# One weight sum of the block products made by an adding DMA, and the first weight tile of a stretch at 32 bytes

## The chip, the cores and the metric

The kernel runs on one core of a Trainium2 chip. The metric is the device time of one execution in microseconds (us). The kernel before takes 2368.86 us, the median of three runs (2367.31 to 2369.78). The engines are named as in the profile: PE (TensorE, matmuls), PEld (its weight loads), DVE (VectorE), ACT (ScalarE), POOL (GpSimd) and SP (SyncE, which here only issues DMAs).

## The reference

Two layers of an encoder trunk on 512 tokens of width 1024, all in fp32. Each layer is a gated feed-forward block, a mixer (two attentions and a pooling branch, gated and summed), and a second feed-forward block; each is normalised and modulated before and added to `x` after:

```python
def swiglu(h, w_gate, w_up, w_down):
    return (jax.nn.silu(h @ w_gate) * (h @ w_up)) @ w_down

for l in range(DEPTH):                       # DEPTH = 2
    mod = (c_act @ w_ada[l] + b_ada[l]).reshape(B, N_MOD, D_MODEL)
    h = modulate(rms_norm(x, norm_gain[l, 0]), mod[:, 0], mod[:, 1])
    x = x + 0.5 * mod[:, 2][:, None, :] * swiglu(h, ffn_w_gate[l, 0], ffn_w_up[l, 0], ffn_w_down[l, 0])
    ...                                      # the mixer, then the second swiglu
```

The hidden width D_FF is 2816, that is 22 column tiles of 128. The change lies in `h @ w_gate` and `h @ w_up` of the four feed-forward blocks.

## The kernel before

**Precision.** Each fp32 operand is split into a high part of type fp32r and the low rest. A product of two tiles is three matmuls: high by high, high by low, low by high. ACT casts the high part, DVE subtracts to get the low part (`split_to`, L417 and L418; `wchunk`, L310 and L312). The activations h lie transposed in `hhi` and `hlo`, 8 tiles of 128 rows by 512 tokens each.

**A feed-forward block** (`Ffn.run`, L629) goes through its 22 column tiles in three parts of 6, 8 and 8. A part first makes its activations (gate and up products, silu, multiplication), then multiplies them with the rows of `w_down` (`k_outer`, L421). Some column tiles of the first part are done directly, with matmuls of 512 columns (L140 to L142). All others are done in pairs by `seven` (L541), once for gate and once for up.

**`seven`** multiplies the 1024 rows and two column tiles of weights with all tokens as a 2 by 2 block product with seven multiplications instead of eight. Source 0 holds the weight blocks A11 and A12, source 1 holds A21 and A22. It forms four weight sums on DVE, each 128x512 per partition:

- S1 = A21 + A22 (L556), S3 = A11 - A21 (L557)
- S2 = S1 - A11 (L558), S4 = A12 - S2 (L559)

The matching activation sums T1 to T4 are made once for each feed-forward block (`Blocks`). The seven products, in the order in which PE makes them, are A11 B11, A12 B21, S2 T2, S1 T1, S3 T3, S4 B22 and A22 T4. Each is four tiles of three matmuls of 256 columns (`add_product`, L149 to L151), 84 matmuls for a call. Between them ACT copies the accumulators out of PSUM (L572 to L580) and DVE adds them up. The last product may start only after the copy at L580. There are 70 calls, in 11 stretches: three of two calls and eight of eight calls. Before each stretch stand matmuls of 512 columns.

**Where the data lies.** Raw weights are loaded by SP into `raw`, which has two buffers of 512 KB: both are taken by one call, and the loads of the next call wait until DVE has read them. Split weights go into `w` (three buffers) and, for the sums, `ptb` (two buffers). The unsplit sums and the evacuated products `c` take turns in `v2` (four buffers), which at other times takes rows of `w_ada`. `pta` (one buffer) serves the mixer alone. `duo` (L69) gives the place of a split weight inside its tile: `WIDE` = 0 for matmuls of 512 columns, `NARROW` = 16 floats, or 64 bytes, for those of 256. In the program's memory layout the tiles `w`, `b`, `hhi` and `hlo` start at multiples of 128 bytes, the tiles `ptb` 64 bytes past one.

**Halves-wise stages.** The last `k_outer` of each feed-forward block and of each mixer works on token halves, so its matmuls have 256 columns too (L428); its weights are placed at `NARROW` (L447). There are six such stages.

**Order.** The program is written in one order per engine by a planner, from a cost model and the order of the source; each engine then works strictly in order. Modulation work (`mod_step`, `mod_dot`) is slipped in by `side_work`, which `seven` calls ahead of each of its loads.

Of the kernel before, what the change touches and what calls it, by code (L numbers as in the profile page):

```python
# [15 lines left out]
F32 = mybir.dt.float32  # L16
# [3 lines left out]
ALU = mybir.AluOpType  # L20
# [20 lines left out]
def encoder_kernel(tc, xT, c, w_ada, b_ada, gains, w_gate, w_up, w_down, w_qkv, w_f, w_ubg,  # L41
# [22 lines left out]
    def st(shape, dt, tag, bufs):  # L64
        return sb.tile(shape, dt, tag=tag, bufs=bufs, name=nm(tag))

    WIDE, NARROW = 0, 16

    def duo(shape, tag="w", place=WIDE):  # L69

# [214 lines left out]
    def side_work(side=True):  # L285
        mod_flush()
        if quiet[0] > 0:
            quiet[0] -= 1
            if quiet[0] == 0:
                gate.clear()  # L290
        elif side and in_ffn[0] and mod_tag[0] != "raw":
            mod_credit[0] += MOD_RATE[0]
            while mod_credit[0] >= 1.0:
                mod_credit[0] -= 1.0
                mod_pop()

    def wchunk(src, shape, side=True, spare=None, lo_eng=None, place=WIDE):
        lo_eng = lo_eng or nc.vector
        side_work(side)
        raw = st([P] + list(shape), F32, *(("b", NB) if spare else ("raw", NRAW)))  # L300
        last["dma"] = nc.sync.dma_start(raw, src).ins
        if spare == "ptb":
            hi, lo = duo(shape, "ptb")
        elif spare == "b":
            hi = st([P] + list(shape), F32R, "b", NB)
            lo = st([P] + list(shape), F32R, "b", NB)
        else:
            hi, lo = duo(shape, "w", place)
        with behind("scalar"):
            nc.scalar.copy(hi, raw)  # L310
        with behind("vector"):
            lo_eng.tensor_tensor(lo, raw, hi.bitcast(F32), op=ALU.subtract)  # L312
        return hi, lo
# [107 lines left out]
    def k_outer(chunk_src, nch, lhs_rhs, before_last=None):  # L421

        if before_last is None:
            parts, nheld = [(None, slice(0, T), [acc() for _ in range(4)])], 2
        else:
            parts = [(hs, slice(hs * HALF, (hs + 1) * HALF), [b((P, HALF)) for _ in range(4)])  # L428
                     for hs, b in enumerate((mmt, acc))]
            nheld = 3  # L430

        def go(part, j, chunks):
            _, cols, accs = part
            for c, hi, lo in chunks:
                for kk in range(2):
                    a, b, x, y = lhs_rhs(hi[:, kk, :], lo[:, kk, :], 2 * c + kk, j)
                    triple(accs[j], a, b, x[:, cols], y[:, cols], start=(c == 0 and kk == 0),
                           stop=(c == nch - 1 and kk == 1))

        held = []  # L440
        for c in range(nch):
            if before_last is not None:
                if c == nch - 2:
                    quiet[0] = 8
                    before_last()
                quiet[0] = 8
            hi, lo = wchunk(chunk_src(c), (2, T), place=WIDE if before_last is None else NARROW)  # L447
            if c < nch - nheld:
                for part in parts:
                    for j in range(4):  # L450
                        go(part, j, [(c, hi, lo)])
            else:
                held.append((c, hi, lo))
        if before_last is not None:
            quiet[0] = 5
        for part in parts:
            for j in range(4):
                go(part, j, held[:-2])
            for j in range(4):
                go(part, j, held[-2:])  # L460
                yield j, part[0], part[2][j]
# [23 lines left out]
    def minus(o, a, b):  # L485
        nc.vector.tensor_tensor(o, a, b, op=ALU.subtract)  # L486
# [51 lines left out]
            q0, cols = {"T1": (0, FIRST), "T3": (0, SECOND), "T4": (2, FIRST), "T2": (2, SECOND)}[name]  # L538
            return [tuple(part[:, k % 2, cols] for part in self.parts[q0 + k // 2]) for k in range(4)]

    def seven(srcs, blocks, bank):  # L541

        raws = []
        for src in srcs:
            side_work()
            raw = st([P, KD, P], F32, "raw", NRAW)
            last["dma"] = nc.sync.dma_start(raw, src).ins
            raws.append(raw)
        tens = lambda o, a, b, op: nc.vector.tensor_tensor(o, a, b, op=op)
        a11, a12, a21, a22 = raws[0][:, :4], raws[0][:, 4:], raws[1][:, :4], raws[1][:, 4:]  # L550
        ah, al = duo((KD, P), "w", NARROW)
        split_to(ah, al, raws[0])
        bh, bl = duo((4, P), "w", NARROW)
        split_to(bh, bl, a22)
        s12, s34 = st([P, 2, 4, P], F32, "v2", 4), st([P, 2, 4, P], F32, "v2", 4)
        tens(s12[:, 0], a21, a22, ALU.add)  # L556
        minus(s34[:, 0], a11, a21)  # L557
        minus(s12[:, 1], s12[:, 0], a11)  # L558
        minus(s34[:, 1], a12, s12[:, 1])  # L559
        pair12, pair34 = duo((2, 4, P), "ptb"), duo((2, 4, P), "ptb")  # L560
        split_to(*pair12, s12)
        split_to(*pair34, s34)
        lefts = {"A11": [(ah[:, k], al[:, k]) for k in range(4)],
                 "A12": [(ah[:, 4 + k], al[:, 4 + k]) for k in range(4)],
                 "A22": [(bh[:, k], bl[:, k]) for k in range(4)]}
        for name, pair, i in (("S1", pair12, 0), ("S2", pair12, 1), ("S3", pair34, 0), ("S4", pair34, 1)):
            lefts[name] = [(pair[0][:, i, k], pair[1][:, i, k]) for k in range(4)]
        x, y, w = bank((P, HALF)), bank((P, HALF)), bank((P, HALF))
        c = st([P, 4, HALF], F32, "v2", 4)
        go = lambda o, left, right, start: add_product(o, lefts[left], blocks.operand(right), start)  # L570
        go(x, "A11", "B11", True)
        nc.scalar.copy(c[:, 0], x)  # L572
        go(y, "A12", "B21", True)
        tens(c[:, 0], y, c[:, 0], ALU.add)
        go(x, "S2", "T2", False)
        nc.scalar.copy(c[:, 1], x)
        go(w, "S1", "T1", True)
        nc.scalar.copy(c[:, 2], w)
        go(x, "S3", "T3", False)
        nc.scalar.copy(c[:, 3], x)  # L580
        go(w, "S4", "B22", False)
        tens(c[:, 1], w, c[:, 1], ALU.add)
        tens(c[:, 3], c[:, 2], c[:, 3], ALU.add)
        go(x, "A22", "T4", False)
        return [[c[:, 0:2].rearrange("p a t -> p (a t)")], [x, c[:, 3]]]
# [10 lines left out]
    class Ffn:  # L596
# [32 lines left out]
        def run(self, nxt):  # L629
# [4 lines left out]
            for part, (f0, nf) in enumerate(parts):  # L634
# [40 lines left out]
                    n += 1  # L675
                if not opening:
                    blocks.finish()
                while n < nf:
                    both = [apply(p, AF.Silu)
                            for p in seven([w_gate[l, s, f0 + n + i] for i in range(2)], blocks, acc)]  # L680
                    ups = seven([w_up[l, s, f0 + n + i] for i in range(2)], blocks, mmt)
                    for i, sg in enumerate(both):
                        acts.append(self.act(n + i, None, ups[i], sg))
                    n += 2
# [646 lines left out]
```

## Time and profile before

| | |
|---|---|
| median of three runs | 2368.86 us |
| the profiled execution's own time | 2370.22 us |
| its span (first to last instruction) | 2368.4 us |
| PE busy | 2335.2 us (99%) |
| DVE busy | 1770.8 us (75%) |
| ACT busy | 1197.2 us (51%) |
| POOL busy | 326.4 us (14%) |
| HBM read | 312.16 MB, 134 GB/s with what is written |

A row of a timeline has the start, the duration, the engine, the line, the operation, the tiles (written <- read), the shape and a count; in square brackets the idle time of the engine before it and what ended that. A row of a group has the count, then busy time and mean duration in ns, then the idle time before and who ended it. A row of a window has its length, then the busy time of each engine with the number of instructions that touch it, the granted clock, the share of time in which the DMA engines were busy, and GB/s. Matmuls are pipelined, so one matmul's duration is longer than the step from its start to the start of the next; the pace is read from the starts.

### The profile page before, as it was taken

The numbers are of one execution on the slowest core, as the hardware profiler recorded it, in microseconds if no ns is written. First come the engines' busy times: TensorE is split into PE (matmuls) and PEld (weight loads), VectorE is DVE, ScalarE is ACT, GpSimd is POOL, SyncE is SP. The second block draws the span as 40 slices with busy tenths as digits, with TensorE's granted clock in tenths as the row PEclk, the third lists the DMA queues.
The fourth block names the chain that finished last, engine by engine and source line by source line (L and its number), as shares of the span: only waits on it lengthen the run. The fifth ranks groups of instructions, "written<-read, shape, count | busy, mean of one in ns | idle before, by whom it ended". The sixth has DMA issues, their size and how long they took to land.

```text
span 2368.4 us, 37435 instructions
## 1 busy us (share of the span) xinstructions
PE 2335.2 (99%) x14322; PEld 2075.8 (88%) x14322; DVE 1770.8 (75%) x3147; ACT 1197.2 (51%) x2097; POOL 326.4 (14%) x433
## 2 busy tenths in 40 slices
PE   7999999999999999999999999999999999999999
PEld 5898998878888898989999989888788888999898
DVE  8887866787686577878687878677866855878583
ACT  5353555676632353635553536456765324636262
POOL 3000011244411100000100000112543211000000
PEclk9999999999999999999999999999999999999999
DMA  8535342333355524353415353533333654143233
GB/s 292 182 107 187 101 167 88 105 99 110 122 199 202 188 71 161 116 187 99 152 63 178 101 185 107 187 107 99 99 122 106 221 199 167 63 142 108 98 100 107
DMA packets 117976, 325.18 MB, mean 137 GB/s; under 512 B 11650, under 2 KB 13826, under 8 KB 117796
## 3 DMA queue, kind: packets, MB, share of 16 engines
q1 hardware_dynamic: 115106, 314.38, 39.9%
q0 software_dynamic: 2688, 8.39, 1.2%
q8 instruction: 113, 1.85, 0.3%
q14 instruction: 67, 0.55, 0.1%
q10 hardware_dynamic: 2, 0.00, 0.0%
HBM read 312.16 MB, written 6.38 MB: 134 GB/s over the span
## 4 chain that ended last, share of the span: by engine, by line
PE 85%; DVE 9%; ACT 3%; DMA 2%; issue 2%; SPq 0%; ACTq 0%; DVEq 0%; POOL 0%; POOLq 0%
PE acc L140 16%; PE acc L142 16%; PE acc L141 16%; PE mm L151 4%; PE mm L149 4%; PE mm L150 4%; PE acc L149 4%; PE acc L151 4%; PE acc L150 4%; PE mm L140 3%; PE mm L142 3%; PE mm L141 3%; PE mm L1020 1%; DVE w L418 1%; DVE v L486 1%
## 5 line engine op out<-in xcount | busy, mean ns | idle before, releaser
L312 DVE TENSOR_TENSOR w<-raw,w 128x1024 fp32r<-128x1024 f32 x247 | 313.2, 1271 | 161.6 <-ACT w L310 161.3
L310 ACT CAST w<-raw 128x1024 fp32r<-128x1024 f32 (+1 forms) x255 | 264.3, 1040 | 273.4 <-PE acc L142 187.5
L140 PE MATMUL acc<-b,w 128*128 128x512 f32 (+1 forms) x960 | 359.8, 375 | 0.0
L141 PE MATMUL acc<-b,w 128*128 128x512 f32 (+1 forms) x960 | 356.3, 371 | 0.0
L142 PE MATMUL acc<-b,w 128*128 128x512 f32 (+1 forms) x960 | 356.1, 371 | 0.0
L142 PEld LDWEIGHTS acc<-b,w 128*128 128x128 f32 x960 | 180.4, 188 | 31.6
L140 PEld LDWEIGHTS acc<-b,w 128*128 128x128 f32 x960 | 180.3, 188 | 30.3
L141 PEld LDWEIGHTS acc<-b,w 128*128 128x128 f32 x960 | 180.6, 188 | 29.8
L417 ACT CAST ptb<-v 128x1024 fp32r<-128x1024 f32 x140 | 146.6, 1050 | 100.8 <-DVE v L486 62.0
L418 DVE TENSOR_TENSOR ptb<-v,ptb 128x1024 fp32r<-128x1024 f32 x140 | 170.7, 1222 | 33.2 <-ACT ptb L417 32.7
L140 PE MATMUL acc<-hhi,w 128*128 128x512 f32 x480 | 191.9, 401 | 2.4 <-ACT hhi L747 1.7
L142 PE MATMUL acc<-hhi,w 128*128 128x512 f32 x480 | 188.8, 393 | 2.6 <-DVE w L312 2.6
L141 PE MATMUL acc<-hlo,w 128*128 128x512 f32 x480 | 188.7, 393 | 0.5 <-DVE hlo L750 0.5
L417 ACT CAST w<-raw 128x1024 fp32r<-128x1024 f32 (+1 forms) x140 | 116.5, 832 | 122.1 <-PE acc L142 56.2
L418 DVE TENSOR_TENSOR w<-raw,w 128x1024 fp32r<-128x1024 f32 (+1 forms) x140 | 133.1, 950 | 13.0 <-ACT w L417 13.0
L140 PE MATMUL acc<-w,hhi 128*128 128x512 f32 x336 | 138.7, 414 | 0.9 <-ACT t L849 0.9
L142 PE MATMUL acc<-w,hlo 128*128 128x512 f32 x336 | 131.9, 392 | 0.0
L141 PE MATMUL acc<-w,hhi 128*128 128x512 f32 x336 | 131.6, 392 | 0.0
L227 DVE CUSTOM_DVE_ANT_0 v<-v,b,badac 128x1024 f32<-128x1024 f32 x87 | 116.8, 1352 | 10.1 <-DMA v<-in_w_ada_dram 10.1
L149 PE MATMUL acc<-b,ptb 128*128 128x256 f32 x420 | 118.3, 282 | 0.0
L150 PE MATMUL acc<-b,ptb 128*128 128x256 f32 x420 | 117.8, 280 | 0.0
L151 PE MATMUL acc<-b,ptb 128*128 128x256 f32 x420 | 117.7, 280 | 0.0
(312 smaller groups left out, 6583.7 us busy)
## 6 DMA issues: line engine op xcount, KB each, us to landing
raw<-in_w_down_dram SPq DMA_DIRECT2D x88, 512.0 KB, 4.1
v<-in_w_ada_dram SPq DMA_DIRECT2D x87, 512.0 KB, 5.1
raw<-in_w_up_dram SPq DMA_DIRECT2D x82, 512.0 KB, 3.6
raw<-in_w_gate_dram SPq DMA_DIRECT2D x79, 512.0 KB, 3.6
b<-in_w_ada_dram SPq DMA_DIRECT2D x57, 512.0 KB, 4.7
raw<-in_w_ubg_dram SPq DMA_DIRECT2D x56, 512.0 KB, 3.6
raw<-in_w_qkv_dram SPq DMA_DIRECT2D x42, 512.0 KB, 3.7
raw<-in_w_branch_dram SPq DMA_DIRECT2D x24, 512.0 KB, 3.7
```

The lines of the kernel that those rows point to most:

```text
L140: mm(o, lh, rh, start=start, stop=False)
L141: mm(o, lh, rl, start=False, stop=False)
L142: mm(o, ll, rh, start=False, stop=stop)
L149: mm(o, lh, rh, start=start and k == 0, stop=False, skip_group_check=True)
L150: mm(o, lh, rl, start=False, stop=False, skip_group_check=True)
L151: mm(o, ll, rh, start=False, stop=k == 3, skip_group_check=True)
L227: dot = nc.vector.tensor_tensor_reduce(out=raw, in0=raw, in1=silc[0], scale=1.0, scalar=badac[:, l, j, d:d + 1], op0=ALU.mult, op1=ALU.add ...
L310: nc.scalar.copy(hi, raw)
L312: lo_eng.tensor_tensor(lo, raw, hi.bitcast(F32), op=ALU.subtract)
L417: nc.scalar.copy(hi, src)
L418: nc.vector.tensor_tensor(lo, src, hi.bitcast(F32), op=ALU.subtract)
L486: nc.vector.tensor_tensor(o, a, b, op=ALU.subtract)
```

## The change

In `seven`:

- A21 is no longer loaded into `raw`. SP loads it straight into the place of S1, in a `v2` buffer (256 KB), and an adding DMA from POOL's queue then adds A22 to it there (256 KB). The addition on DVE goes. With `s34` gone from `v2`, the sums S1, S2 of successive calls alternate with the products `c`.
- SP then loads the top tile (A11, A12; 512 KB) and A22 alone (256 KB) into `raw`.
- S3 is formed as A22 - S2, which is the same as A11 - A21, after S2 instead of before it.
- S3 and S4 lie in `pta` instead of `v2`.

Placement: the first weight tile of a stretch (the split A11, A12 of its first gate call) and the first weight chunk of each halves-wise stage stand at `ENTRY` = 8 floats, or 32 bytes, instead of 64 bytes.

```diff
-    WIDE, NARROW = 0, 16
+    WIDE, ENTRY, NARROW = 0, 8, 16
...
-            hi, lo = wchunk(chunk_src(c), (2, T), place=WIDE if before_last is None else NARROW)
+            hi, lo = wchunk(chunk_src(c), (2, T), place=WIDE if before_last is None else NARROW if c else ENTRY)
...
-    def seven(srcs, blocks, bank):
-
-        raws = []
-        for src in srcs:
-            side_work()
-            raw = st([P, KD, P], F32, "raw", NRAW)
-            last["dma"] = nc.sync.dma_start(raw, src).ins
-            raws.append(raw)
+    def seven(srcs, blocks, bank, place=NARROW):
+
+        top, low = srcs
+        s12, s34 = st([P, 2, 4, P], F32, "v2", 4), st([P, 2, 4, P], F32, "pta", 1)
+        nc.sync.dma_start(s12[:, 0], low[:, :4])
+        nc.gpsimd.dma_start(s12[:, 0], low[:, 4:], accum_op=ALU.add)
+        side_work()
+        r0 = st([P, KD, P], F32, "raw", NRAW)
+        last["dma"] = nc.sync.dma_start(r0, top).ins
+        side_work()
+        a22 = st([P, 4, P], F32, "raw", NRAW)
+        last["dma"] = nc.sync.dma_start(a22, low[:, 4:]).ins
         tens = lambda o, a, b, op: nc.vector.tensor_tensor(o, a, b, op=op)
-        a11, a12, a21, a22 = raws[0][:, :4], raws[0][:, 4:], raws[1][:, :4], raws[1][:, 4:]
-        ah, al = duo((KD, P), "w", NARROW)
-        split_to(ah, al, raws[0])
+        a11, a12 = r0[:, :4], r0[:, 4:]
+        ah, al = duo((KD, P), "w", place)
+        split_to(ah, al, r0)
         bh, bl = duo((4, P), "w", NARROW)
         split_to(bh, bl, a22)
-        s12, s34 = st([P, 2, 4, P], F32, "v2", 4), st([P, 2, 4, P], F32, "v2", 4)
-        tens(s12[:, 0], a21, a22, ALU.add)
-        minus(s34[:, 0], a11, a21)
         minus(s12[:, 1], s12[:, 0], a11)
+        minus(s34[:, 0], a22, s12[:, 1])
         minus(s34[:, 1], a12, s12[:, 1])
...
+                place = ENTRY
                 while n < nf:
                     both = [apply(p, AF.Silu)
-                            for p in seven([w_gate[l, s, f0 + n + i] for i in range(2)], blocks, acc)]
+                            for p in seven([w_gate[l, s, f0 + n + i] for i in range(2)], blocks, acc, place)]
+                    place = NARROW
                     ups = seven([w_up[l, s, f0 + n + i] for i in range(2)], blocks, mmt)
```

## The prediction

> **What bounds the kernel now.** I read the page first (busy time, clock, chain), then the exact windows of the block products, then single matmul starts in order of time, then the groups with their waits.
>
> ```profile
> span 2368.4 us, 37435 instructions
> ...
> PE 2335.2 (99%) x14322; PEld 2075.8 (88%) x14322; DVE 1770.8 (75%) x3147; ACT 1197.2 (51%) x2097; POOL 326.4 (14%) x433
> ...
> PEclk9999999999999999999999999999999999999999
> ...
> PE 85%; DVE 9%; ACT 3%; DMA 2%; issue 2%; SPq 0%; ACTq 0%; DVEq 0%; POOL 0%; POOLq 0%
> ```
>
> TensorE is busy for 99% of the span at the full granted clock and carries 85% of the chain. Work taken from another engine pays only where TensorE waits for it or runs at a slower pace. The change touches two kinds of stage: the 70 calls of `seven` (84 matmuls of 256 columns each) and the six halves-wise outer products.
>
> ```profile
> core 0: us, PE busy (x) PEld busy (x) DVE busy (x) ACT busy (x) POOL busy (x), PEclk, DMA share, GB/s
> 123.62:202.81 79.19, 78.95 (x674) 78.75 (x672) 69.50 (x105) 46.64 (x80) 0.00 (x0) 1.00 0.42 133
> ...
> 1290.48:1370.65 80.17, 79.08 (x674) 78.59 (x672) 69.00 (x103) 46.22 (x80) 0.00 (x0) 1.00 0.41 130
> ...
> sum 695.24, PE 689.72 PEld 686.73 DVE 597.36 ACT 401.50 POOL 0.00; mean PE 62.70 PEld 62.43 DVE 54.30 ACT 36.50 POOL 0.00
> ```
>
> These windows run from the first block matmul of each of the 11 stretches to the first matmul behind it. Together the 70 calls take 695.24 us, 29% of the span. VectorE is busy for 597.36 us of that, 86%.
>
> The pace inside a stretch has two values. The next rows are the first matmul of a call and of the call after it, early in a stretch and late in the same stretch:
>
> ```profile
> 246.35 0.28 PE L149 MATMUL acc<-hhi,w 128*128 128x256 f32 x1
> 256.25 0.28 PE L149 MATMUL mm<-hhi,w 128*128 128x256 f32 x1
> 295.91 0.28 PE L149 MATMUL mm<-hhi,w 128*128 128x256 f32 x1
> 305.43 0.28 PE L149 MATMUL acc<-hhi,w 128*128 128x256 f32 x1
> ```
>
> A call takes 9.90 us early and 9.52 us late: 117.9 and 113.3 ns per matmul, for the same 84 matmuls on the same kinds of tiles at the same clock. Neither contains a wait. So a call can run 4% faster with no instruction less. What lies between the two is a stall. The largest kind, later in the same stretch:
>
> ```profile
> 313.06 0.69 DVE L486 TENSOR_TENSOR v<-raw,v 128x512 f32<-128x512 f32 x1
> 313.11 1.05 ACT L417 CAST ptb<-v 128x1024 fp32r<-128x1024 f32 x1 [1.62 <-DVE v L486]
> 313.53 0.28 PE L151 MATMUL acc<-hhi,ptb 128*128 128x256 f32 x1
> 314.06 0.37 ACT L580 COPY v<-acc 128x256 f32<-128x256 f32 x1
> 314.48 0.38 PE L149 MATMUL acc<-b,w 128*128 128x256 f32 x1 [0.68 <-ACT v L580]
> ```
>
> The seventh product may not start before ScalarE has copied the accumulator (L580). ScalarE stands in order behind the cast of the next call's first weight sums, which waited 1.62 us for VectorE. Two matmul starts lie 0.95 us apart instead of 0.11.
>
> **The change, part by part.** First the two limits of what the block products can give. At 9.90 us with no stall the 70 calls take 693.0 us, at 9.52 us 666.4 us. Today's 695.24 is 2.2 above the first, because what the stalls cost and what the faster pace behind them saves nearly cancel. The second is 28.8 us away.
>
> *The VectorE addition that goes.* Before, A21+A22 is the instruction of the first row; the second is the cast that waits for VectorE:
>
> ```profile
> L549 DVE TENSOR_TENSOR v<-raw 128x512 f32<-128x512 f32 x70 | 48.2, 689 | 61.3 <-DMA raw<-in_w_gate_dram 58.5 <-DMA raw<-in_w_up_dram 2.7
> L417 ACT CAST ptb<-v 128x1024 fp32r<-128x1024 f32 x140 | 146.6, 1050 | 100.8 <-DVE v L486 62.0 <-ACT v L580 15.4 <-PE mm L151 11.9
> ```
>
> It takes 0.689 us x 70 = 48.2 us, and VectorE stands idle for another 61.3 us before it, nearly all until the second raw tile has landed. Afterwards S2 = sum - A11 needs only the first raw tile and the sum made by DMA. The remaining three VectorE subtractions are as many as before, 128x512 each (S3 reads A22 and S2 in place of A11 and A21), so 0 for them. The cast at 313.11 could start at least 0.69 us sooner, and up to 0.69 + 61.3/35 = 2.4 us sooner in a gate call, where the landing is waited for. The stall above, 0.95 - 0.11 = 0.84 us, lies between these two. I take it that half of the stall time goes; what is left I set at 4.5 us for all 70 calls (about 0.4 us in 11 of them), with 0 and 10 us as ends.
>
> *The transfers that come.* Per call: a plain 256 KB load on SP, an adding 256 KB load on POOL's queue behind it, the 512 KB top tile, a 256 KB load of A22; 1.25 MB where there was 1 MB. No adding DMA is in the trace. The nearest rows:
>
> ```profile
> raw<-in_w_gate_dram SPq DMA_DIRECT2D x79, 512.0 KB, 3.6
> x_dram<-xv POOLq DMA_DIRECT2D x8, 512.0 KB, 3.1
> strip<-in_rel_dram SPq DMA_DIRECT2D x16, 256.0 KB, 2.6
> b<-in_w_qkv_dram SPq DMA_DIRECT2D x6, 512.0 KB, 7.1
> raw<-in_w_down_dram SPq DMA_DIRECT2D x88, 512.0 KB, 4.1
> ...
> L1176 POOL DMA_DIRECT2D x_dram<-xv x8: 561/572/751, 343.1 to 1542.6; - x8
> ```
>
> Low end: it lands like a plain 256 KB load, 2.6 us. High end: like the slowest 512 KB row, 7.1 us, since it moves its bytes both in and out. I take 4, nearer the low end because the POOL-issued row of twice its size takes 3.1. With its forerunner and the issue on POOL the chain is 2.6 + 0.57 + 4 = 7.2 us; at the high end 4.1 (the w_down loads' median landing) + 0.75 + 7.1 = 12.0. Its cover:
>
> ```profile
> 294.13 1.23 DVE L418 TENSOR_TENSOR ptb<-v,ptb 128x1024 fp32r<-128x1024 f32 x1 [0.44 <-ACT ptb L417]
> 301.81 1.62 SPq L547 DMA_DIRECT2D raw<-in_w_up_dram  x2
> 311.14 0.68 DVE L549 TENSOR_TENSOR v<-raw 128x512 f32<-128x512 f32 x1
> ```
>
> The call whose sum VectorE forms at 311.14 has the slot that the call two before it gives up at 294.13 + 1.23 = 295.36. In SP's queue its first load stands ahead of the raw tiles issued at 301.81, so it can leave at 295.4 and the sum is whole at 302.6, at worst 307.4, against a need at 311.1. Cost 0, with 3.7 us to spare at the high end. POOL is idle in all eleven windows (POOL 0.00 in the sum), so nothing stands before or behind the DMA in its queue. The extra 0.25 MB fits a stage whose DMA engines are busy for 0.40 of the time. S3 and S4 now lie in a tile with one buffer (`pta`); its next writer comes one call, 9.5 us, later. Cost 0.
>
> *The first tile of a stretch at 32 bytes.* It moves no instruction. That the place of a weight tile matters is in the trace. Weights from `b` tiles stand at multiples of 128 bytes, from `ptb` and narrow `w` tiles 64 bytes past one:
>
> ```profile
> 862.87 0.29 PE L141 MATMUL mm<-hlo,b 128*128 128x256 f32 x1
> ...
> 863.79 0.28 PE L140 MATMUL mm<-hhi,ptb 128*128 128x256 f32 x1
> ...
> 864.13 0.28 PE L142 MATMUL mm<-hhi,b 128*128 128x256 f32 x1
> ...
> 866.29 0.28 PE L142 MATMUL mm<-hhi,b 128*128 128x256 f32 x1
> ...
> 2034.34 0.28 PE L141 MATMUL mm<-hlo,b 128*128 128x256 f32 x1
> 2034.46 0.28 PE L141 MATMUL mm<-hlo,ptb 128*128 128x256 f32 x1
> ...
> 2035.63 0.28 PE L142 MATMUL mm<-hhi,b 128*128 128x256 f32 x1
> ```
>
> Three steps from `ptb` take 0.34 us, 113 ns each; eighteen from `b` take 2.16, 120 each. The `ptb` tiles at 863.79 came after `b` tiles (862.87) and ran at 113; at 2034.46 the same switch left them at 1.17/10 = 117. So 64-byte tiles keep one of two paces, and a tile at another place, or a stall, can flip it. Every stretch is entered from 512-column tiles at 0 straight into tiles at 64 and starts at 117.9. With 24 matmuls at 32 bytes between, the pace may flip at the entry. Best case: all 70 calls at 113.3. Worst: the tile itself runs at 120 like `b` and nothing flips: 11 x 24 x 2 ns = 0.5 us lost. I take the flip, at a price of 11 x 24 x 6.7 ns (120 against 113.3) = 1.8 us for its own matmuls, because a switch of places flipped it at 863 and stalls flip it in the calls.
>
> The halves-wise stages get the same entry tile:
>
> ```profile
> 825.26:841.50 16.24, 16.24 (x139) 1.00 0.33 98
> ...
> 1515.80:1533.72 17.92, 16.75 (x139) 1.00 0.45 147
> ...
> 2342.25:2364.75 22.50, 22.50 (x193) 1.00 0.23 71
> ...
> sum 105.50, PE 104.33; mean PE 17.39
> ```
>
> Their six windows hold 5 x 138 + 191 = 881 matmuls. Without the 1.7 us that the row of 1515.80 has over its like, they take 103.8 at 117.9; at 113.3 it is 99.8: 4.0 less.
>
> Sum against the profiled execution's own 2370.22: -28.8 + 4.5 + 1.8 - 4.0 = -26.5, so 2343.7. That execution lies 1.4 above the median of 2368.86, so the median becomes about **2342**.
>
> **Rivals.** *Entry without effect.* The stalls go, but with them the faster pace that followed them. Then 693.0 + at most 2 in the calls: -2.2 to 0, 2367 to 2369. For it: each of the eleven entries now starts at the slow pace, and 2034.46 stayed there. Against it: the flip at 863. The Trainium skill ("SBUF — State Buffer", "Who interferes with whom") gives TensorE two independent read ports, for moving operand and weights, and says it never waits for anyone; by that a tile's place could not matter and this rival would be certain. The rows at 113, 118 and 120 ns speak against so strict a reading.
>
> *Flip that doesn't last.* The stretches start fast, but remaining stalls in gate calls flip some back. If half the calls stay slow, half of 28.8 + 4.0 is lost: about 2355. For it: VectorE has 597.36 - 48.2 = 549 us to do in 666.4, still 82%.
>
> *The transfers get in each other's way: slower.* Three loads on SP and one on POOL share the queues; if the 512 KB tile lands behind the new 256 KB pieces, VectorE's wait of 61.3 us grows by up to 2.6 us in 35 gate calls, 91 us, while it is spared 48.2. In proportion the stalls go from some 10 us (a dozen like the one shown) to 17, with the entry tile without effect: 693.0 + 17 against 695.24, and 3 us at the eleven starts, where modulation rows load beside: +18, about 2387. At a milder 1.5 us it is even; it decides from there. For it: b<-in_w_qkv at 7.1 us for 512 KB shows what crowding does. Against it: a DMA share of 0.40 and the 3.7 us to spare.
>
> The Trainium skill ("SBUF — State Buffer", "SBUF: two separate sides") warns that a GpSimd-issued DMA starves while VectorE runs a two-port instruction, and, by inference, excepts the two-input kind that fills these stages. If it starved all the same, by one 1.23 us instruction per DMA, the chain of 12.0 would be 13.2, still inside the 15.7 from 295.4 to 311.1.
>
> **How the numbers follow.** Forecast 0.52 (2334 to 2350), flip that doesn't last 0.13, no effect 0.20, in each other's way 0.15. 0.2% of the time, 4.7 us, is about what a measurement of this kernel can tell from no change: faster is the first two and a little of the third, 0.66; same the rest of the third, 0.19; slower 0.15. The range must leave out no more than 2 in 10: low end 2334 (all gains, no stall left, some 34 less), high end 2371, which takes in the third case and leaves the fourth out.
>
> **What would show it.** Right: the eleven windows sum to about 673 us, calls of 9.52 us from the first of a stretch on, the idle time before VectorE's first subtraction of a call well under 61.3 us, L580 waits under 2 us. Wrong: calls of 9.9 us at the start of a stretch (entry), a VectorE subtraction that waits for POOL's DMA (chain too slow), or the raw loads of w_gate landing later than 3.6 us (crowding).

## The result, and the profile after

The changed kernel takes **2474.01 us** (median of four runs, 2473.56 to 2482.07) against 2368.32 us of the kernel before on the same chip: a ratio of **1.0452** (95% interval 1.0439 to 1.0466), 105.7 us slower. The forecast was 2342 us. The profiled execution took 2474.18 us. In `after`, `seven` begins at L541; the load of A21 is L545, the adding DMA L546, the top tile L549, A22 L552, the copies out of PSUM L574 to L582. S2, S3 and S4 all go through the helper `minus` (L486).

From the page of the kernel after (span, busy time, bytes, chain of waits):

```profile
span 2472.4 us, 37580 instructions
...
PE 2356.6 (95%) x14322; PEld 2088.0 (84%) x14322; DVE 1727.8 (70%) x3077; ACT 1195.4 (48%) x2097; POOL 388.2 (16%) x503
...
HBM read 330.51 MB, written 6.38 MB: 136 GB/s over the span
...
PE 63%; DMA 16%; DVE 12%; ACT 5%; issue 3%; SPq 0%; POOLq 0%; POOL 0%; ACTq 0%; DVEq 0%
```

VectorE has lost 43 us of work, as intended, but DMA, 2% of the chain before, now carries 16% of it. The windows of the eleven stretches (length, then busy time by engine, granted clock, DMA share, GB/s; the second of the eight long ones, the first short one, the sum):

```profile
260.71:356.46 95.75, 83.04 (x673) 81.46 (x672) 64.00 (x99) 46.23 (x80) 6.05 (x7) 0.95 0.44 122
924.34:943.50 19.16, 19.16 (x170) 19.16 (x168) 15.06 (x24) 9.97 (x18) 0.89 (x1) 1.00 0.55 168
...
sum 800.94, PE 712.96 PEld 700.90 DVE 554.78 ACT 399.94 POOL 51.80; mean PE 64.81 PEld 63.72 DVE 50.43 ACT 36.36 POOL 4.71
```

800.94 - 695.24 = 105.70 us: the 70 calls hold the whole loss. TensorE is idle for 88 us of them (5.5 before). A short stretch of two calls can still be free of stalls: 19.16 us, which is 9.64 for the first call and 9.52 for the second. So the entry tile does what was forecast, and the loss grows with the length of a stretch. The group that waits:

```profile
L149 PE MATMUL mm<-b,ptb 128*128 128x256 f32 x420 | 126.3, 301 | 61.0 <-ACT v L574 50.9
L486 DVE TENSOR_TENSOR v<-v,raw 128x512 f32<-128x512 f32 x70 | 48.4, 692 | 178.9 <-DMA v<-in_w_up_dram 91.9
```

The first row is the start of each tile of the third to fifth products in half of the calls; TensorE waits 61.0 us before it, 50.9 of them for the copy at L574. The second row is S2 = sum - A11. VectorE stands idle for 178.9 us before it, nearly all until the sum has landed. Followed through one call, in the timelines of SP, POOL and VectorE, in order of time:

```profile
298.01 0.33 SPq L549 DMA_DIRECT2D raw<-in_w_gate_dram  x1
298.91 0.33 SPq L552 DMA_DIRECT2D raw<-in_w_gate_dram  x1
299.29 0.42 SPq L545 DMA_DIRECT2D v<-in_w_gate_dram  x1
303.50 0.86 POOL L546 DMA_DIRECT2D v<-in_w_gate_dram  x1 [10.41 <-DMA v<-in_w_gate_dram]
307.67 0.69 DVE L486 TENSOR_TENSOR v<-v,raw 128x512 f32<-128x512 f32 x1 [3.13 <-DMA v<-in_w_gate_dram]
308.40 0.69 DVE L486 TENSOR_TENSOR pta<-raw,v 128x512 f32<-128x512 f32 x1
309.15 0.33 SPq L549 DMA_DIRECT2D raw<-in_w_up_dram  x1
309.34 0.68 DVE L486 TENSOR_TENSOR pta<-raw,v 128x512 f32<-128x512 f32 x1
310.05 0.33 SPq L552 DMA_DIRECT2D raw<-in_w_up_dram  x1
310.43 0.42 SPq L545 DMA_DIRECT2D v<-in_w_up_dram  x1
```

This is **a loop**. On SP the load of A21 stands behind the top tile and A22 of its own call. It lands and POOL issues the adding DMA 4.21 us later; S2 starts 4.17 us after that. S3 gives up the raw buffer of A22 at 309.09 and S4 that of the top tile at 310.02; only then can SP issue the next two raw loads, and the next A21 behind them, at 310.43. One turn takes 310.43 - 299.29 = 11.14 us, and TensorE needs 9.52. This turn is one of the quicker ones: within the eight long stretches the issues of A21 lie 10.1 to 13.5 us apart, with a median of 11.6. In a stretch of eight calls TensorE catches up with the loop in the second call and waits in nearly every call from then on.

What that does on TensorE, in the call that uses the sum of 307.67 (timelines of PE and ACT):

```profile
310.67 0.28 PE L151 MATMUL acc<-hhi,w 128*128 128x256 f32 x1
312.12 0.62 ACT L417 CAST b<-t 128x512 fp32r<-128x512 f32 x1 [0.94 <-DVE t L626]
312.65 0.37 ACT L574 COPY v<-acc 128x256 f32<-128x256 f32 x1
313.07 0.54 PE L149 MATMUL acc<-b,ptb 128*128 128x256 f32 x1 [2.12 <-ACT v L574]
313.40 0.42 PE L150 MATMUL acc<-b,ptb 128*128 128x256 f32 x1
313.62 0.42 PE L151 MATMUL acc<-b,ptb 128*128 128x256 f32 x1
```

The third product may not start before the copy at L574, which stands on ScalarE behind casts that waited for VectorE, which had waited for the sum. And behind the wait TensorE does not resume at its pace: the next steps are 0.22 us instead of 0.11. In 14 of the 70 calls such steps of 213 ns follow, 208 of them when the matmul starts are counted: 208 x 0.1 us, some 21 us.

### The profile page after: what moved, and what is told of

It reads as the page before. It is cut to its first block, busy times and chain, and to the rows that moved or that the text cites. A ratio compares the mean times of both kernels' runs of the same rounds, so it can differ in the third digit from the quotient of the medians.

```text
span 2472.4 us, 37580 instructions
## 1 busy us (share of the span) xinstructions
PE 2356.6 (95%) x14322; PEld 2088.0 (84%) x14322; DVE 1727.8 (70%) x3077; ACT 1195.4 (48%) x2097; POOL 388.2 (16%) x503
## 4 chain that ended last, share of the span: by engine, by line
PE 63%; DMA 16%; DVE 12%; ACT 5%; issue 3%; SPq 0%; POOLq 0%; POOL 0%; ACTq 0%; DVEq 0%
PE acc L140 15%; PE acc L142 15%; PE acc L141 15%; DMA v<-in_w_up_dram 7%; DMA v<-in_w_gate_dram 4%; PE mm L142 3%; PE mm L140 3%; PE mm L141 3%; DVE pta L486 2%; DMA raw<-in_w_gate_dram 2%; PE mm L149 2%; PE mm L151 2%; PE mm L150 2%; DVE v L486 2%; DMA raw<-in_w_up_dram 1%
## 5 line engine op out<-in xcount | busy, mean ns | idle before, releaser
L149 PE MATMUL mm<-b,ptb 128*128 128x256 f32 x420 | 126.3, 301 | 61.0 <-ACT v L574 50.9
L486 DVE TENSOR_TENSOR v<-v,raw 128x512 f32<-128x512 f32 x70 | 48.4, 692 | 178.9 <-DMA v<-in_w_up_dram 91.9
L149 PE MATMUL acc<-b,ptb 128*128 128x256 f32 x420 | 124.2, 296 | 27.0 <-ACT v L574 26.7
L149 PEld LDWEIGHTS mm<-b,ptb 128*128 128x128 f32 x420 | 84.4, 201 | 69.3 <-ACT v L574 57.4
L417 ACT CAST ptb<-v 128x1024 fp32r<-128x1024 f32 x70 | 73.6, 1051 | 132.4 <-DVE v L486 132.4
L467 DVE SCALAR_TENSOR_TENSOR xv<-acc,badac,xv 128x512 f32<-128x512 f32 (+1 forms) x112 | 77.2, 690 | 68.9 <-PE acc L142 68.9
```

The lines of the kernel that those rows point to most:

```text
L149: mm(o, lh, rh, start=start and k == 0, stop=False, skip_group_check=True)
L417: nc.scalar.copy(hi, src)
L467: nc.vector.scalar_tensor_tensor(x, acc_j, gate, x, op0=ALU.mult, op1=ALU.add)
```

## The experiments

Calls is the sum of the eleven windows in the profiled execution (in bound_after other matmuls stand between the block products, and the sum is that of the pieces). Each ratio is to the kernel before as it ran beside that kernel, with medians from 2367.09 to 2368.78 us. The table is followed by the edits, in the order in which they were run.

| kernel | us | ratio to before (95%) | calls, us |
|---|---|---|---|
| before | 2368.32 | 1 | 695.24 |
| the change | 2474.01 | 1.0452 (1.0439 to 1.0466) | 800.94 |
| sum_first | 2402.32 | 1.0136 (1.0085 to 1.0187) | 727.64 |
| entry_only | 2362.18 | 0.9973 (0.9952 to 0.9994) | 687.52 |
| dma_only | 2482.22 | 1.0468 (1.0408 to 1.0529) | 808.52 |
| no_second | 2342.44 | 0.9892 (0.9867 to 0.9918) | 669.23 |
| plain_second | 2417.43 | 1.0206 (1.0186 to 1.0227) | 743.18 |
| sum_first_late_act | 2369.22 | 1.0005 (0.9995 to 1.0014) | 692.78 |
| entry_copy_first | 2362.20 | 0.9973 (0.9963 to 0.9983) | 691.65 |
| early_after | 2471.99 | 1.0439 (1.0423 to 1.0455) | 794.14 |
| early_64 | 2473.43 | 1.0438 (1.0421 to 1.0456) | 797.57 |
| early_vec | 2582.36 | 1.0905 (1.0888 to 1.0921) | 910.60 |
| pool_add | 2364.81 | 0.9985 (0.9976 to 0.9994) | 691.63 |
| entry_pool_sum | 2387.10 | 1.0071 (1.0059 to 1.0084) | 711.27 |
| sum_ahead | 2440.03 | 1.0306 (1.0292 to 1.0320) | 770.83 |
| sum_ahead_64 | 2446.73 | 1.0329 (1.0314 to 1.0343) | 771.76 |
| **bound_ahead** | **2347.83** | **0.9914 (0.9899 to 0.9928)** | 673.56 |
| bound_after | 2461.04 | 1.0394 (1.0376 to 1.0411) | 781.71 |
| bound_ahead_64 | 2366.37 | 0.9995 (0.9985 to 1.0005) | 688.02 |

**sum_first**: the A21 load goes ahead of the raw loads on SP.

```diff
-        nc.sync.dma_start(s12[:, 0], low[:, :4])
+        half = nc.sync.dma_start(s12[:, 0], low[:, :4]).ins
...
+        with tc.issue_after(half):          # the same for a22
             last["dma"] = nc.sync.dma_start(r0, top).ins
```

> The changed kernel with one thing ordered otherwise: on SP the load of A21 into the place of S1 is issued ahead of the two raw loads of its own call (in the changed kernel the planner put it behind them). All the work is the same. Theory (a loop through the DMAs: raw buffers free, r0 and A22 issued, only then A21, 3.6 to 5 us to land, then the adding DMA of 4.1 us, then S2 to S4, which free the raw buffers; about 11.2 us a call against 9.52 us of PE): the A21 load now leaves one call earlier, the idle time of DVE before S2 (178.9 us) falls under 40 us, the calls return to 9.5 to 9.7 us, and the time is 2335 to 2350 us. Rival 1 (the adding DMA or the number of transfers is itself too slow or crowds the queues): landings stay late, 2440 us or more. Rival 2 (the single buffer of S3 and S4 sets the pace): 2400 us or more, with DVE waiting on ACT's cast of that buffer.

2402.32 us: most of the loss is gone, 72 of 106 us, but not all. Groups of VectorE and TensorE, then both timelines in one of the gate calls:

```profile
L486 DVE TENSOR_TENSOR v<-v,raw 128x512 f32<-128x512 f32 x70 | 48.1, 687 | 38.1 <-DMA raw<-in_w_gate_dram 29.3 <-DMA v<-in_w_gate_dram 4.4 <-DMA raw<-in_w_up_dram 4.3
L151 PE MATMUL acc<-b,ptb 128*128 128x256 f32 x420 | 115.7, 285 | 34.0 <-DVE ptb L418 34.0
...
291.65 0.68 DVE L486 TENSOR_TENSOR v<-v,raw 128x512 f32<-128x512 f32 x1
292.25 0.69 DVE L628 TENSOR_TENSOR t<-v,t 128x512 f32<-128x512 f32 x1
...
295.92 1.22 DVE L418 TENSOR_TENSOR ptb<-v,ptb 128x1024 fp32r<-128x1024 f32 x1
297.20 0.38 PE L151 MATMUL acc<-b,ptb 128*128 128x256 f32 x1 [1.40 <-DVE ptb L418]
```

The wait for sums is gone (178.9 to 38.1 us, and of that only 4.4 for a sum). In its place TensorE waits for the low part of S1 and S2: the split at 295.92 stands behind the activation products of the pair before (L628) on VectorE. The planner had changed VectorE's order along with SP's: in the change this split, at 310.28, stood ahead of the products, at 311.41. The time lies inside the second rival's range, but its mechanism isn't there: VectorE waits only 5.5 us in all ahead of S3 and S4, 4.5 of them for a raw tile.

**entry_only** and **dma_only**: the two halves of the change apart.

```diff
+    WIDE, ENTRY, NARROW = 0, 8, 16          # entry_only: before, with the placement alone
...
-                place = ENTRY               # dma_only: after, without the placement
+                place = NARROW
```

> The kernel before with the placement alone: first weight tile of a stretch and first chunk of a halves-wise stage at 32 bytes; sums, loads and order as before. Theory (the entry tile alone sets the pace of a stretch at 113.3 ns): calls of 9.90 us become 9.52 to 9.64 us from the first of a stretch, while the waits for the VectorE addition stay and grow a little because PE asks earlier: 2340 to 2358 us. Rival (the pace came from the stalls of the adding DMA, not from the place): as before, 2367 to 2370 us, with calls of 9.90 us.

> The changed kernel with every tile back at 64 bytes, so the adding DMA, the separate A22 and the moved S3 alone. Theory (the loop makes the loss; the place only sets the pace until the first stall): first calls of a stretch 9.90 instead of 9.64 us (11 times 0.3 us) and the halves-wise stages 4 us longer: 2476 to 2486 us, stalls as in the changed kernel. Rival (part of the loss comes from the 32-byte tile): 2450 us or less.

entry_only gains 0.27%, some 6 us, less than its theory gave: 687.52 - 666.4 - 1.3 leaves 20 us of stalls, 18.4 of them at the last copy, where the kernel before has 8.9. dma_only carries the whole loss, and some 8 us more. So the adding DMA half is the cause.

**no_second**: no adding DMA.

```diff
-        nc.gpsimd.dma_start(s12[:, 0], low[:, 4:], accum_op=ALU.add)
```

> The changed kernel without the adding DMA, so that S1 is A21 alone (the addition of A22 is left out, and with it 18.4 MB of reading); issue order on SP as in the changed kernel, r0, A22, A21. Theory: the loop loses one of its two landings (4.1 us, and POOL's issue of 0.9 us), about 6.5 us a call, under PE's 9.52 us: no stall is left, 2332 to 2348 us. Rival (it is not the chain of two landings but the single buffer of S3 and S4, or the planner's order on DVE and ACT): stalls stay, 2400 us or more.

2342.44 us. The sum of its windows:

```profile
sum 669.23, PE 668.14 PEld 667.90 DVE 564.38 ACT 399.60 POOL 0.00; mean PE 60.74 PEld 60.72 DVE 51.31 ACT 36.33 POOL 0.00
```

All calls but one take 9.52 us (9.64 at an entry). The separate A22, the moved S3, the single `pta` buffer and the order r0, A22, A21 on SP are all still in it, so none of them costs by itself.

**plain_second**: POOL copies instead of adding.

```diff
-        nc.gpsimd.dma_start(s12[:, 0], low[:, 4:], accum_op=ALU.add)
+        nc.gpsimd.dma_start(s12[:, 0], low[:, 4:])
```

> The changed kernel with POOL's second DMA as a plain copy over the place of S1 instead of an adding one (so S1 is A22 alone, the addition is left out; bytes, queues, waits and order as in the changed kernel). Theory (two landings one behind the other in the loop): the loop shrinks only by the difference between the adding DMA's landing (4.1 us) and a plain one from POOL, at most 1 us a call: 2430 to 2470 us. Rival (it is the adding that is slow): near the kernel without the second DMA, under 2380 us.

2417.43 us, better than the theory said and far from the rival. The DMA rows (median us from issue to landing), first of the changed kernel, then of this one:

```profile
v<-in_w_gate_dram POOLq DMA_DIRECT2D x35, 256.0 KB, 4.1
```

```profile
v<-in_w_gate_dram POOLq DMA_DIRECT2D x35, 256.0 KB, 2.9
```

Adding takes 1.2 us more than copying. The median turn, from one A21 to the next in the long stretches, falls from 11.6 to 10.8 us. That is still longer than 9.52, so about half of the loss stays.

**sum_first_late_act** and **entry_copy_first**: two order edges against the stalls that were left.

```diff
+        mid(low12)     # sum_first_late_act: the pair's activation products, behind the split of the next call's sums
...
+        with tc.issue_after(copied.pop()):  # entry_copy_first: cast of the next sums behind the last copy
+            split_to(*pair12, s12)
```

> The kernel with the A21 load ahead of the raw loads, and the activation products of a finished pair (three multiplications and two subtractions on VectorE, 2.9 us, ahead of S3, S4 and the split of S1 and S2 of the next gate call) put behind that split. Theory (what was left in sum_first is VectorE's order: these products lengthen the time until the raw buffers come free and until the low part of S2 is there, 1.68 us of stall in a gate call): the stalls at the second tile of S2 T2 go, 2342 to 2362 us. Rival (the sum itself still comes late): no change, 2390 to 2405 us, with VectorE's S2 waiting for the DMA into v.

> The kernel before with the 32-byte entry tile and one order edge: ScalarE's cast of the next call's S1 and S2 stands behind the last copy of the call (L580) instead of ahead of it; sums on VectorE, no adding DMA. Theory (in entry_only the only stall left is this copy behind that cast, 0.5 to 1 us in 22 gate calls, 687.5 us in the calls against 667.7 without a stall): 2342 to 2352 us. Rival (the cast then comes too late for the next call and the stall moves to S2 T2): 2358 to 2370 us.

The first brings another 33 us and ends at the time of before: better than the rival, short of the theory, with small waits of 0.1 to 0.9 us left in 50 of the 70 calls. The second gains nothing over entry_only: the stall moved to the third product, as its rival said, and short waits turned the pace back. Three rows of its second call, at the step into the third product:

```profile
136.75 0.38 PE L149 MATMUL mm<-b,ptb 128*128 128x256 f32 x1
136.97 0.28 PE L150 MATMUL mm<-b,ptb 128*128 128x256 f32 x1
...
137.32 0.28 PE L150 MATMUL mm<-b,ptb 128*128 128x256 f32 x1
```

One step of 0.22 us, and from there three steps take 0.35 us, 117 ns each, and so in the next three calls. So a wait of 0.1 us can also flip the pace to the slow side.

**early_after**, **early_64**, **early_vec**: the whole preparation of a call written ahead of the products of the call before.

```diff
+    def ahead(srcs, place=NARROW):          # the four DMAs, the split of A11 and A12, S2, S3, S4
...
+                    coming += load()        # call k + 1, then
                     both = [apply(p, AF.Silu) for p in seven(mine, blocks, acc)]
```

> The changed kernel with the preparation of a call (its four DMAs, the split of A11 and A12, S2, S3, S4) written ahead of the products of the call before it instead of behind them; what is computed is the same. SP then issues A21 of a call between r0 and A22 of the call before it, one call ahead. Theory (only the place of the sum in the loop costs, not the sum itself): the sum is whole before S2 asks, calls of 9.5 to 9.7 us, 2340 to 2356 us. Rival (the adding DMA costs something wherever it stands, or VectorE's and ScalarE's orders are what is left): like sum_first_late_act or worse, 2365 to 2400 us.

> The same as early_after with every tile at 64 bytes (no entry tile), instruction for instruction in the same order. Theory: without stalls the pace stays at what a stretch is entered with, 9.90 us a call, 20 to 30 us more than early_after: 2365 to 2382 us. Rival (the place has no effect where nothing stalls): the same time as early_after.

> The kernel before with the 32-byte entry tile and the same early preparation, sums on VectorE from two loaded 512 KB tiles, no adding DMA. Theory of a full VectorE (48.2 us more of it than with the adding DMA): better than entry_only, but some stalls left, 2346 to 2360 us. Rival (the adding DMA is needed for nothing): 2340 to 2345 us, the same as early_after.

All three theories missed; only the rival of early_64, the same time as early_after, came out. Waits of SP's queue in early_after (us in total, times, longest):

```profile
SPq L552 <- DVE w L418: 275.6, 56, 12.3
```

The split of A22 had stayed with the products, so the raw buffer of A22 came free only there; the load of the next A22 waited for it at the head of SP's queue, and all others behind it. In early_vec SP waits for the same splits for 430.1 us. The edit made a new loop and says nothing on the old one. That early_64 equals early_after shows only that the place is worth nothing where every call stalls.

**pool_add** and **entry_pool_sum**: S1 added by POOL's arithmetic, in the changed kernel (no adding DMA) and in the kernel before.

```diff
-        nc.gpsimd.dma_start(s12[:, 0], low[:, 4:], accum_op=ALU.add)
...
+        nc.gpsimd.tensor_tensor(s12[:, 0], s12[:, 0], a22, op=ALU.add)   # entry_pool_sum: a21, a22
```

> The changed kernel with the adding DMA replaced by an addition on POOL: A21 is loaded into the place of S1 as in the changed kernel, in the same place of SP's queue (behind r0 and A22 of its own call), and POOL adds the A22 that stands in the raw buffer (128x512 takes POOL 1.66 us in the row of L1206). Theory (the second landing in the loop is what costs, not the moved S3, the single buffer of S3 and S4, the split loads or the order): the loop is 4.1 + 0.9 - 1.7, some 3.3 us shorter, under PE's 9.52 us: 2338 to 2352 us, calls of 9.5 to 9.6 us. Rival (POOL's addition and VectorE slow each other, or the other parts of the change cost as well): 2360 us or more.

> The kernel before with the 32-byte entry tile and S1 on POOL instead of VectorE; A21 and A22 loaded as one 512 KB tile as before. Theory (in entry_only VectorE's 48.2 us for S1 are what makes S2 late): 2338 to 2352 us. Rival (S1 starts only when the second 512 KB tile has landed and takes 1 us longer on POOL, so S2 and the cast come later still): 2358 to 2375 us.

pool_add recovers the whole loss with the A21 load where the change has it: the second landing is what the loop can't bear. It doesn't reach 2342. What stands against it shows in two rows of the same moment:

```profile
289.31 1.29 POOL L558 TENSOR_TENSOR v<-v,raw 128x512 f32<-128x512 f32 x1 [7.29 <-DVE b L418]
289.35 2.34 DVE L418 TENSOR_TENSOR w<-raw,w 128x1024 fp32r<-128x1024 f32 x1
```

The split takes 2.34 us beside POOL's addition; without one it takes 1.23, and the mean of its group over both shapes is 1182 ns here and 956 ns in no_second. The Trainium skill ("SBUF — State Buffer", "Who interferes with whom") says that a VectorE instruction with two SBUF inputs contends with a GpSimd instruction that reads SBUF; the trace agrees. VectorE is busy for 603.71 us of the calls here and for 564.38 in no_second; that this alone makes the difference was not tested by itself. In entry_pool_sum POOL's addition waits for a 512 KB tile first, and the kernel is slower than before, by more than its rival gave (2387.10 against 2358 to 2375).

**sum_ahead** and **sum_ahead_64**: only the two DMAs of a sum are written one call earlier.

```diff
+                    if pairs:
+                        sums.append(sum_of(pairs[0][1]))   # A21 on SP, adding A22 on POOL
+                    return seven(mine, blocks, bank, place, sums.pop(0))
```

> The changed kernel with only the two DMAs of a sum (A21 on SP, the adding A22 on POOL) written one call earlier, ahead of the raw loads and products of the call before; every instruction and byte as in the changed kernel. Theory (the adding DMA costs nothing where its two landings are off the loop of the raw buffers): VectorE's idle time before S2 waiting for a sum falls from 150 us to under 15, calls of 9.52 to 9.65 us, 2340 to 2352 us. Rival (the adding DMA costs something in itself, by its writes into SBUF or by crowding the loads): 2360 us or more, as in sum_first_late_act.

> The same kernel with every tile at 64 bytes, in the same order on every engine. Theory (where little stalls, a stretch keeps the pace it is entered with): calls of 9.90 us until the first stall, 12 to 30 us more than sum_ahead, the halves-wise stages 4 us of it. Rival (the entry tile gives nothing where the sum comes early): within 5 us of sum_ahead.

Missed again: 2440.03 us, and 2446.73 with every tile at 64 bytes, 6.7 more, which lies between that run's theory and its rival. Group and timeline of VectorE in sum_ahead:

```profile
L486 DVE TENSOR_TENSOR v<-v,raw 128x512 f32<-128x512 f32 x70 | 48.5, 692 | 188.7 <-DMA raw<-in_w_up_dram 91.5 <-DMA v<-in_w_gate_dram 50.9 <-DMA raw<-in_w_gate_dram 41.4
...
299.76 0.69 DVE L486 TENSOR_TENSOR v<-v,raw 128x512 f32<-128x512 f32 x1 [4.02 <-DMA raw<-in_w_up_dram]
300.37 1.22 DVE L418 TENSOR_TENSOR ptb<-v,ptb 128x1024 fp32r<-128x1024 f32 x1
```

VectorE now waits mostly for the raw tile: with the sum early, the planner put S2 ahead of the split of the call before (300.37), so VectorE blocks on a tile that is not there yet. Place and order were still mixed, so the last three kernels fix the order.

**bound_ahead**, **bound_after**, **bound_ahead_64**: VectorE and ScalarE bound, instruction by instruction, to the order that they have in no_second; applied to sum_ahead, to the changed kernel, and to sum_ahead with every tile at 64 bytes.

```diff
+        for a, b in zip(row, row[1:]):      # row: one engine's instructions in the order of no_second
+            tc.add_manual_dep(b, a.name, mb.DependencyInfo(mb.DependencyClass.NoSync, mb.DependencyReason.DATA),
+                              reason="order")
```

> The kernel of sum_ahead (the two DMAs of a sum written one call earlier) with VectorE and ScalarE bound, instruction by instruction, to the order that they have in no_second, so that the only difference from no_second is the adding DMA (all of the computation is there) and where A21 stands on SP. Theory (the place in the loop and the order that follows from it make the whole loss; the adding DMA off the loop is free): stalls gone as in no_second, calls of 9.52 us, 2340 to 2350 us. Rival (the adding DMA costs something in itself, or 18.4 MB more reading slows the loads): 2358 us or more, with waits for raw tiles or sums.

> The changed kernel with VectorE and ScalarE bound to the same order of no_second, its DMAs where they are (A21 behind r0 and A22 of its own call). Theory (the order cannot help while two landings stand in the loop): 2430 to 2485 us, VectorE idle before S2 for 150 us or more, waiting for the DMA. Rival (the planner's order on VectorE and ScalarE is the cause): under 2380 us.

> The kernel of bound_ahead with every tile at 64 bytes, in the same order on every engine, so only the place of the entry tiles differs. Theory (where nothing stalls, a stretch keeps the pace it is entered with): calls of 9.90 us in place of 9.52, 70 x 0.38 less the 1.3 of the entry tiles, that is 20 to 26 us more with the few stalls that flip it, and 4 us in the halves-wise stages: 2366 to 2378 us. Rival (the entry tile gives nothing): within 5 us of bound_ahead, 2343 to 2353 us.

bound_ahead takes **2347.83 us**, ratio 0.9914 (0.9899 to 0.9928): faster than both kernels by more than the intervals, with every adding DMA and byte of the change in it. Its span, the sum of its windows, the group of S2, one sum through SP, POOL and VectorE (L582 and L583 are its two DMAs, L525 is `minus`), and the starts of two calls:

```profile
span 2343.9 us, 37698 instructions
...
sum 673.56, PE 671.01 PEld 669.77 DVE 566.30 ACT 400.60 POOL 43.12; mean PE 61.00 PEld 60.89 DVE 51.48 ACT 36.42 POOL 3.92
...
L525 DVE TENSOR_TENSOR v<-v,raw 128x512 f32<-128x512 f32 x70 | 48.0, 685 | 41.8 <-DMA raw<-in_w_gate_dram 34.3 <-DMA v<-in_w_gate_dram 7.3
...
281.44 0.33 SPq L582 DMA_DIRECT2D v<-in_w_gate_dram  x1
284.96 0.86 POOL L583 DMA_DIRECT2D v<-in_w_gate_dram  x1 [8.26 <-DVE b L457]
296.46 0.68 DVE L525 TENSOR_TENSOR v<-v,raw 128x512 f32<-128x512 f32 x1
...
254.15 0.28 PE L188 MATMUL mm<-hhi,w 128*128 128x256 f32 x1
...
263.67 0.28 PE L188 MATMUL acc<-hhi,w 128*128 128x256 f32 x1
```

The adding DMA is issued 11.5 us before S2 asks, VectorE waits only 7.3 us in all for a sum, and a call takes 9.52 us. bound_after has the same order on VectorE and ScalarE and the DMAs in the loop: 2461.04 us. Its group of S2:

```profile
L525 DVE TENSOR_TENSOR v<-v,raw 128x512 f32<-128x512 f32 x70 | 48.5, 693 | 189.6 <-DMA v<-in_w_up_dram 83.2 <-DMA v<-in_w_gate_dram 77.2 <-DMA raw<-in_w_gate_dram 29.2
```

VectorE waits 160.4 us for sums. So this order alone doesn't help; the place of the two landings decides, and the order has to fit it. One thing more differs in bound_after: the planner let the products of neighbouring calls take turns on TensorE, which it doesn't do in bound_ahead or no_second.

bound_ahead_64 differs from bound_ahead in the place of the entry tiles alone:

```profile
sum 688.02, PE 686.15 PEld 685.40 DVE 570.73 ACT 404.66 POOL 43.14; mean PE 62.38 PEld 62.31 DVE 51.88 ACT 36.79 POOL 3.92
...
256.88 0.28 PE L188 MATMUL mm<-hhi,w 128*128 128x256 f32 x1
...
266.77 0.28 PE L188 MATMUL acc<-hhi,w 128*128 128x256 f32 x1
```

9.89 us a call, until a stall flips it in some stretches: 18.5 us more in the medians. The profiled execution is the quickest of ten, 2361.39 us; its windows show 14.5 of them.

## Why the prediction was wrong, step by step

- **What bounds, and the limits of the calls.** Right. No stall at the fast pace was put at 666.4 us plus the entry; no_second measures 669.23.
- **The VectorE addition.** Right in kind. 4.5 us of stalls were to be left; bound_ahead has 673.56 - 667.7 = 5.9. In the change itself VectorE's wait ahead of its first subtraction rose, from 61.3 to 178.9 us, for the reason in the next item.
- **The transfers that come: the step that failed.** The adding DMA's duration was right (4 us taken, 4.1 to 4.2 measured). The plain load ahead of it was put at 2.6 us and took 3.6 to 3.8 in the median, and the chain of 7.2 us came out at 307.67 - 299.29 = 8.4, inside the range given. Wrong was the sentence "In SP's queue its first load stands ahead of the raw tiles issued at 301.81, so it can leave at 295.4". It took the order of the source for the order of issue. The planner put A21 behind both raw loads of its own call, and these wait for the raw buffers that S3 and S4 of the call before give up. So the 3.7 us to spare didn't exist, and the cost was not 0: the calls take 800.94 - 673.56 = 127 us more than in bound_ahead, where the landings stand off the loop and VectorE and ScalarE have an order to match. That the next raw loads hang on S2, S3 and S4, and these on the sum, was not said at all. Drawn as a loop, the prediction's own chain of 7.2 us and the 2.8 us from S2 to the next A21 (307.67 to 310.43) already make 10.0 against 9.52. Why the planner chose that order was not tested by itself. That writing the sum ahead of the products `c`, which share `v2` with it, puts A21 a call earlier (sum_ahead) fits an explanation by the turn in which slots are given out.
- **POOL idle, DMA share, `pta`.** Right: raw tiles land after 3.6 us as before, at a DMA share of 0.46 instead of 0.41 over the windows, and `pta` costs nothing in no_second and bound_ahead.
- **The entry tile.** Right: eleven entries flip, at 9.64 - 9.52 = 0.12 us each, 1.3 us where 1.8 was put. In the pair with few stalls the place is worth 18.5 us (28.8 less 1.8 was the forecast against calls that are all slow; in bound_ahead_64 stalls made 17 calls fast as well). The Trainium skill ("SBUF — State Buffer", "Who interferes with whom") would have it worth nothing, since TensorE waits for nobody; this pair is against that.
- **The halves-wise stages.** Mis-sized: 4.0 us were put for six of them. The five with 138 matmuls give 81.32 - 80.55 = 0.8, and the sixth goes from 22.50 to 21.89 us: 1.4 in all. Windows of bound_ahead and of bound_ahead_64 (length, PE busy, clock, DMA):

```profile
343.87:360.25 16.38, 16.38 (x140) 1.00 0.42 130
821.81:837.69 15.88, 15.88 (x140) 1.00 0.65 165
...
1978.98:1995.45 16.47, 16.18 (x140) 1.00 0.59 161
sum 80.55, PE 80.27; mean PE 16.05
```

```profile
sum 81.32, PE 81.32; mean PE 16.26
```

  Three of the five go from 16.26 to 15.9 us. In the stage at 343.87 a step of 0.25 us turns the pace back to 118 ns. The one at 1978.98 keeps the fast pace but has a step of 0.56 us. And the 48 matmuls of each entry chunk run at 118 ns themselves, which the forecast counted as fast: 6 x 48 x 4.6 ns = 1.3 us.
- **The rivals.** The slower one had the right sign with the wrong mechanism: it had raw tiles landing behind the new pieces, and they land on time. "A VectorE subtraction that waits for POOL's DMA (chain too slow)", given as what would show the forecast wrong, is what the trace shows. With the sum where the prediction had it, and an order to match, its 2342 is missed by 6 us (bound_ahead).

## What to carry to other kernels

Before a transfer is called hidden, draw the loop in which it stands: which buffers the loads behind it wait for, who frees them, and whether that one waits for the transfer itself; then compare one turn of the loop with the time of a call. The place in an engine's queue is read from the compiled order, not from the source, and the planner changes it when a slower producer is put in. Two landings one behind the other take 8.4 us here, nearly a whole call, so such a chain has to start a call or more ahead (15 us ahead of S2 in the rows of bound_ahead), and the order of the engines that use it has to be moved with it.

## What the runs showed that was not expected

- **Half pace behind a wait.** Behind waits of 2.1 to 4.0 us, in 14 calls of the changed kernel, matmuls run in steps of 213 ns, the mean clock of a stretch falls to 0.94, and TensorE loses some 21 us on top of the waits. The Trainium skill ("TensorE: Matmul & The Clock Gate", "Part 1: The HAM clock gate") has two rates, the lower one at 1.2 GHz; worked out from it, 256 columns take an estimated 213.3 ns, and the trace agrees. The same section of the Trainium skill has the lower rate follow an idle window of about 3.4 us. Here waits of 2.1 to 2.4 us were enough in some calls (the call shown above: 2.4 us between two starts), while one of 3.8 us was followed by none.
- **The pace of 113.3 or 117.9 ns is a state.** A tile at 32 bytes sets it to the fast one (its own matmuls take 118), a wait of 0.1 us can set it to the slow one (entry_copy_first), and without a wait it lasts for a whole stretch (bound_ahead, bound_ahead_64).
- **An adding DMA** of 256 KB lands 4.1 us after its issue on POOL, a plain one from the same queue after 2.9.
